# Banded attention's scores from whole 128-row operands: both parts of a head's q stacked in one tile, both parts of k twice

## The chip, the cores and the metric

One core of a Trainium2 chip runs the whole kernel in one launch. The metric is the device time of one execution in microseconds. The engines are TensorE (PE, with its weight loads PEld), VectorE (DVE), ScalarE (ACT), GpSimd (POOL) and SyncE (SP, which here only issues transfers).

## The reference

The kernel computes the trunk of a hybrid encoder: 2 layers, 512 tokens, 1024 channels, all in fp32. Each layer projects the tokens once for two token mixers and their gates, runs mixer A (banded grouped-query attention), mixer B (three groups of dilated banded attention), merges them by gates, and goes on with a projection, a LayerNorm, a squared-ReLU MLP, a gated per-layer embedding and another LayerNorm. What matters here is mixer A:

```python
A_Q_HEADS, A_KV_HEADS, HEAD_DIM, A_WINDOW = 8, 2, 64, 128
qa = _rope(qa.reshape(bsz, seq, A_Q_HEADS, HEAD_DIM), cos, sin)    # rotary, first 16 of 64 channels
ka = _rope(ka.reshape(bsz, seq, A_KV_HEADS, HEAD_DIM), cos, sin)
oa, _ = _banded_attention(qa, ka, va, A_WINDOW, a_sink)

def _banded_attention(q, k, v, window, sink=None):
    ...
        s = jnp.einsum('nqkgd,nskd->nkgqs', qj.astype(jnp.float32) * scale, kj)
        ...
        s = jnp.where(mask, s, -jnp.inf)          # |i - j| <= 128
        m = jnp.maximum(jnp.max(s, axis=-1), sink_b)
        e = jnp.exp(s - m[..., None])
        denom = jnp.sum(e, axis=-1) + jnp.exp(sink_b - m)
        o = jnp.einsum('nkgqs,nskd->nqkgd', e, vj) / denom
```

A query block of 128 tokens sees its own block and its two neighbours: 256 keys at the ends of the sequence and 384 inside.

## The kernel before

**Products in two parts.** TensorE multiplies a reduced form of fp32. Each operand is therefore split in two: hi, the operand rounded to that form (a copy by ACT, L222), and lo, what is left (a subtraction by DVE, L223). A product takes three passes, hi·hi, lo·hi and hi·lo, which add up in one PSUM bank (`mm3`, L272 to L276). Weights arrive in fp32 by DMA (`wst`) and are split the same way into `whi` and `wlo`, 128x1024 at a time, in three buffers each.

**Channels on partitions.** q and k lie with the channel on the partition, two heads of 64 channels to a tile of 128 rows and 512 tokens. The four q tiles of mixer A hold heads i and i + 4, which use the two heads of the one k tile. `rope` (L365) turns a projection into such a tile: DVE shuffles the partitions of a PSUM bank (L368), DVE multiplies the bank by the cosines (L369), POOL multiplies the shuffled tile by the sines (L370), DVE adds (L371), and ACT and DVE split the sum (L222, L223) into a `qh` and a `ql` tile, of which there are 5 each for q and k of both mixers.

**The scores.** `pair_scores` (L429) makes the scores of one query block for the two heads of a tile: three passes, in each of which the two heads' matmuls follow one another, one on rows 0 to 63 and one on rows 64 to 127, into two PSUM banks. They are named sa, in mixer B sb. DVE then adds the mask and takes the maximum in one custom instruction (`masked`, L426), ACT exponentiates (L422), PE transposes the probabilities (`probs_T`, L411), ACT and DVE split them (ptha, ptla), and PE multiplies them with the values (`weighted`, L437 and L438) into the one bank oa. A head's sum leaves that bank by a copy of ACT and an addition of DVE (`join`, L442 and L443: fa); PE spreads the reciprocal denominators (L456: rsa), DVE scales (L457) and splits into oah and oal.

**PSUM.** There are 3 banks for projections (mm), 2 for scores (s), 2 for transposes (pt) and 1 for outputs (o). The next use of a bank waits until its last reader is done with it.

**The order of the work.** PE's order in the attention is the one in which the code emits it, under a manual schedule; the code that emits it is a planner (L802 to L835). It goes round: first the ready steps of up to two units (`unit_a` for a q tile of mixer A, `unit_b` and `mix_b` for mixer B), else one step of the filler (`filler`, L746), that is 3 matmuls of a projection listed in FLOW (L34): q tiles 2 and 3 of mixer A, the gates (g), q, k and v of mixer B (qb, kb, vb), and later the branch products. Whether a step is ready it asks a small model of time (`Forecast`, L162): each PE step books its length, `fc.on` books times on ACT, DVE and POOL, and the banks carry the time at which they come free. A score group books 6w/2400 us there, w being its columns. The order on DVE, ACT, POOL and SP is set by a scheduler that sees all instructions.

**Constants.** Cosines, sines, the masks and an identity come as one array. A layer loads all but the identity by one DMA into a tile of 1920 columns (L344 to L353), the identity by another one in layer 0.

Of the kernel before, what the change touches and what calls it, by code (L numbers as in the profile page):

```python
# [20 lines left out]
P = 128  # L21
# [110 lines left out]
CONST_COLS = [("cos", S), ("sin", S), ("ma", 384), ("m0", 256), ("m1", P), ("m2", P), ("id", P)]  # L132


def shape_constants():
# [23 lines left out]
    return np.concatenate([c, s, ma, m0, m1, m2, np.eye(P, dtype=np.float32)], axis=1)  # L159
# [40 lines left out]
def build(nc, tc, plan, down, xT, xN, pT, wst, vec, rows, sink, cst, out):  # L200
# [3 lines left out]
    with ctx:  # L204
# [138 lines left out]
        def attention_block(l, av, rp, vt, OA, OB, begun):  # L343
            ct = rp.tile([P, cst.shape[1] - P], F32, tag="ct", name=f"ct{l}", bufs=1)  # L344
            cc, off = {}, 0
            for n, w in CONST_COLS[:-1]:
                cc[n] = ct[:, off:off + w]
                off += w
# [16 lines left out]
            def rope(ps, dil, name):  # L365
# [6 lines left out]
                hi = av.tile([P, S], F32R, tag="qh", name="qh" + name, bufs=5)  # L372
                lo = av.tile([P, S], F32R, tag="ql", name="ql" + name, bufs=5)
# [60 lines left out]

            def weighted(o, vv, blk, r, pT, cols, first, last):
# [30 lines left out]
            def unit_a(i):  # L466
                q, k = held["qa", i], held["ka"]
# [8 lines left out]
                for j in range(4):  # L476
# [4 lines left out]
                    pair_scores(ss, q, k, slice(j * P, (j + 1) * P), slice(k0, k1), slice(0, w))  # L481
                    fc.pe(6 * w / 2400)
# [8 lines left out]
                held["free_qk"] += 1 + (i == 3)  # L491
# [221 lines left out]
            held = {"P": 0, "qk": 3, "free_qk": 0, "vv": 0}  # L713
# [6 lines left out]
            held["ka"] = rope(kps, False, f"ka{l}")  # L720
# [3 lines left out]
            held["qa", 0] = rope(q0, False, f"qa{l}_0")  # L724
            fc.take("mm")
            held["qa", 1] = rope(q1, False, f"qa{l}_1")
# [19 lines left out]
            def filler():  # L746
                def project(key, sigma_order):
# [3 lines left out]
                    held[key] = rope(ps, sigma_order, "_".join(str(v) for v in (l, *key)))  # L751

                for kind, *idx in FLOW:
                    if kind == "qa":
                        yield from project(("qa", *idx), False)
# [27 lines left out]
            def slots(n, *keys):  # L783
                def ok():
                    if held["P"] + n > 4 or any(k not in held or fc.t < held[k][2] for k in keys):
                        return False
# [546 lines left out]
```

## Time and profile before

| | |
|---|---|
| median of 3 runs | 1546.28 us (1545.49 to 1547.36) |
| the profiled execution | 1546.11 us, its span 1544.3 us |
| busy in the span | PE 1512.5 us, DVE 1091.1, ACT 714.9, POOL 201.3 |
| score matmuls of mixer A (L433, sa) | 192 in both layers, 64 rows each, 256 or 384 columns |
| mixer A's units in layer 0 | about 29 to 118 us of the span |
| mixer A's units in layer 1 | from about 797 us |

The page gives for each engine the time in which it was busy, and the trace the single instructions. In the rows of the timeline stand start, busy time, engine, line, operation, output and inputs by their names, the shape, how many instructions the row holds, and in brackets the idle time ahead of it with what ended it. Matmuls overlap: their busy time is longer than the distance from one to the next, so what a matmul costs PE is read from the starts. In the rows of the waits stand the instruction that waited, the one it waited for, the time in all, how often, and the longest wait.

### The profile page before, as it was taken

Reading aid. Unit: us, or ns where it says so; the run is one execution under the profiler, and the core shown is the slowest. Engines: PE = TensorE matmul, PEld = TensorE weight load, DVE = VectorE, ACT = ScalarE, POOL = GpSimd, SP = SyncE. Lnnn points to the kernel's source line nnn. Section 1 sums busy time; section 2 is a strip of 40 time slices with the busy share of each in tenths; the row PEclk is TensorE's granted clock in tenths of the full one; section 3 lists DMA queues with packets and bytes.
Section 4 is the critical chain, followed back from the end, with each engine's and each line's share of the span. In section 5 each row is a group of like instructions: output and inputs, shape, how many; then the busy total and the mean of one; then the engine's idle time right before and its main releaser. Section 6 shows DMA issues by size and latency. Waiting matters only on the chain.

```text
span 1544.3 us, 19518 instructions
## 1 busy us (share of the span) xinstructions
PE 1512.5 (98%) x7416; PEld 1241.6 (80%) x7416; DVE 1091.1 (71%) x1809; ACT 714.9 (46%) x1186; POOL 201.3 (13%) x159
## 2 busy tenths in 40 slices
PE   8999999999999999999999999999999999999996
PEld 6778788888888888888887778888888888888885
DVE  6778675457568767696877786744575776767868
ACT  4566554344334443444546665543442443444342
POOL 1111110020011120202010101111100211111021
PEclk9999999999999999999999999999999999999998
DMA  6211224245622415142342121255456233241403
GB/s 219 69 55 56 69 69 167 85 127 161 194 71 81 145 49 161 44 151 68 96 149 68 56 69 56 81 164 148 134 140 207 68 98 121 71 134 55 150 1 95
DMA packets 46317, 162.19 MB, mean 105 GB/s; under 512 B 5648, under 2 KB 5776, under 8 KB 46224
## 3 DMA queue, kind: packets, MB, share of 16 engines
q1 hardware_dynamic: 43200, 152.00, 30.7%
q0 software_dynamic: 2448, 8.91, 3.1%
q8 instruction: 58, 0.95, 0.3%
q14 instruction: 35, 0.29, 0.1%
q10 hardware_dynamic: 576, 0.04, 0.0%
HBM read 155.16 MB, written 4.19 MB: 103 GB/s over the span
## 4 chain that ended last, share of the span: by engine, by line
PE 89%; DVE 6%; ACT 2%; DMA 2%; issue 1%; SPq 0%; ACTq 0%; DVEq 0%
PE dn L1004 17%; PE ps_up L275 8%; PE ps_up L274 8%; PE ps_up L276 8%; PE wo L281 2%; PE wo L282 2%; PE wo L280 2%; PE pg L282 2%; PE pg L281 2%; PE pg L280 2%; DVE wlo L223 1%; PE sa L433 1%; PE sb L433 1%; PE pta L411 1%; PE ps_start L274 1%
## 5 line engine op out<-in xcount | busy, mean ns | idle before, releaser
L223 DVE TENSOR_TENSOR wlo<-wst,whi 128x1024 fp32r<-128x1024 f32 (+1 forms) x171 | 220.2, 1291 | 149.5 <-ACT whi L222 144.8
L222 ACT CAST whi<-wst 128x1024 fp32r<-128x1024 f32 (+1 forms) x171 | 175.5, 1026 | 295.2 <-PE ps_up L275 115.5
L274 PE MATMUL ps_up<-xhi,whi 128*128 128x512 f32 x512 | 199.2, 389 | 0.0
L275 PE MATMUL ps_up<-xlo,whi 128*128 128x512 f32 x512 | 199.2, 389 | 0.0
L276 PE MATMUL ps_up<-xhi,wlo 128*128 128x512 f32 x512 | 199.2, 389 | 0.0
L977 POOL TENSOR_TENSOR hr<-r 128x512 f32<-128x512 f32 x64 | 102.2, 1597 | 551.4 <-ACT r L969 531.0
L274 PEld LDWEIGHTS ps_up<-xhi,whi 128*128 128x128 f32 x512 | 96.1, 188 | 20.0
L276 PEld LDWEIGHTS ps_up<-xhi,wlo 128*128 128x128 f32 x512 | 96.1, 188 | 20.0
L275 PEld LDWEIGHTS ps_up<-xlo,whi 128*128 128x128 f32 x512 | 96.1, 188 | 19.9
L222 ACT CAST whi<-raw 128x1024 fp32r<-128x1024 f32 x56 | 58.0, 1052 | 97.0 <-PE ps_up L275 57.6
L222 ACT CAST dhi<-raw 128x1024 fp32r<-128x1024 f32 x56 | 58.7, 1052 | 81.9 <-PE dn L1004 60.0
L1023 DVE TENSOR_TENSOR y<-y,dn 128x512 f32<-128x512 f32 x96 | 65.1, 682 | 38.7 <-PE dn L1004 38.7
L957 DVE TENSOR_TENSOR raw<-raw,raw 128x1024 f32<-128x1024 f32 x64 | 86.4, 1349 | 0.2
L223 DVE TENSOR_TENSOR wlo<-raw,whi 128x1024 fp32r<-128x1024 f32 x56 | 68.2, 1221 | 14.1 <-ACT whi L222 14.1
L223 DVE TENSOR_TENSOR dlo<-raw,dhi 128x1024 fp32r<-128x1024 f32 x56 | 69.2, 1239 | 5.4 <-ACT dhi L222 5.2
L1004 PE MATMUL dn<-whi,smh 128*128 128x512 f32 x128 | 50.1, 394 | 0.7 <-DVE y L1023 0.7
L282 PE MATMUL pg<-bhi,xlo 128*128 128x512 f32 x128 | 49.9, 390 | 0.9 <-DVE xlo L901 0.9
L1004 PE MATMUL dn<-wlo,smh 128*128 128x512 f32 x128 | 50.6, 395 | 0.2
L1004 PE MATMUL dn<-whi,sml 128*128 128x512 f32 x128 | 49.9, 390 | 0.0
L280 PE MATMUL pg<-bhi,xhi 128*128 128x512 f32 x128 | 49.9, 390 | 0.0
L1004 PE MATMUL dn<-dhi,smh 128*128 128x512 f32 x128 | 49.9, 390 | 0.0
L1004 PE MATMUL dn<-dlo,smh 128*128 128x512 f32 x128 | 49.8, 389 | 0.0
(834 smaller groups left out, 3878.4 us busy)
## 6 DMA issues: line engine op xcount, KB each, us to landing
wst<-wst SPq DMA_DIRECT2D x187, 512.0 KB, 3.6
raw<-wst SPq DMA_DIRECT2D x64, 512.0 KB, 4.3
y<-rows POOLq DMA_DIRECT2D x14, 512.0 KB, 7.8
row<-rows SPq DMA_DIRECT2D x7, 512.0 KB, 9.4
wst<-wst SPq DMA_DIRECT2D x10, 256.0 KB, 3.6
xs<-xT SPq DMA_DIRECT2D x8, 256.0 KB, 5.0
y<-xN SPq DMA_DIRECT2D x4, 512.0 KB, 6.2
kept<-y SPq DMA_DIRECT2D x4, 512.0 KB, 2.8
```

Of the source, the lines that this page charges most:

```text
L222: nc.scalar.copy(hi, src)
L223: nc.vector.tensor_tensor(lo, src, hi.bitcast(F32), ALU.subtract)
L274: nc.tensor.matmul(ps, w[0][:, s], x[0], start=start, stop=False, skip_group_check=part)
L275: nc.tensor.matmul(ps, w[0][:, s], x[1], start=False, stop=False, skip_group_check=part)
L276: nc.tensor.matmul(ps, w[1][:, s], x[0], start=False, stop=stop, skip_group_check=part)
L280: nc.tensor.matmul(ps, x[0], w[0][:, c], start=start, stop=False)
L281: nc.tensor.matmul(ps, x[0], w[1][:, c], start=False, stop=False)
L282: nc.tensor.matmul(ps, x[1], w[0][:, c], start=False, stop=stop)
L957: nc.vector.tensor_tensor(to, to, other, ALU.add)
L977: nc.gpsimd.tensor_tensor(h.rearrange("p s t -> p (s t)"), r, r, ALU.mult)
L1004: nc.tensor.matmul(ps[s], a[:, k, tok], w[b][:, cols], start=first and not (k or m), stop=k == 3 and m == 2, skip_group_check=True)
L1023: return nc.vector.tensor_tensor(to, to, ps, ALU.subtract if n in (2, 4, 5) else ALU.add)
```

## The change

The scores of mixer A no longer pair two heads of 64 rows. For each head, q is kept as one tile of 128 rows that holds the hi part in one half and the lo part in the other half, and k as two tiles, the hi part in both halves and the lo part in both halves. One matmul with k's hi tile gives hi·hi + lo·hi, a second one with k's lo tile gives hi·lo and also lo·lo, which was left out before. So a group takes 4 matmuls of 128 rows (`whole_scores`) in place of 6 of 64 rows. Mixer B still uses `pair_scores`.

For that, `rope` splits the rotated tile in pieces of 64 rows: a q tile by 2 pieces on ACT and 2 on DVE in place of 1 and 1, the k tile by 4 and 4 in place of 1 and 1. The planner books 4w/2400 us for a group, the rotation's steps for such tiles by the table ROPE, and the buffers of `qh` and `ql` go from 5 to 6, with the limit in the filler. The constants lie in four tiles that share the 12 buffers of the gates (11 before): four DMAs in place of one, each layer. In the changed kernel the lines of the attention stand 37 to 42 further on: L426 is L463, L433 is L475, L437 and L438 are L479 and L480, L411 is L448, L368 is L376, L369 is L377, L371 is L379, L456 and L457 are L498 and L499, L442 and L443 are L484 and L485.

```diff
-CONST_COLS = [("cos", S), ("sin", S), ("ma", 384), ("m0", 256), ("m1", P), ("m2", P), ("id", P)]
+CONST_COLS = [[("cos", S)], [("sin", S)], [("ma", 384), ("m1", P)], [("m0", 256), ("m2", P)], [("id", P)]]
...
-            ct = rp.tile([P, cst.shape[1] - P], F32, tag="ct", name=f"ct{l}", bufs=1)
+                ct = rp.tile([P, S], F32, tag="gate", name=f"ct{l}_{i}", bufs=12)
+                cts.append((ct[:, :n], cst[:, off:off + n]))
...
             def load_constants():
-                nc.sync.dma_start(ct, cst[:, :off])
+                for to, what in cts:
+                    nc.sync.dma_start(to, what)
...
-            def rope(ps, dil, name):
+            def rope(ps, dil, name, whole=""):
+                ROPE = (0.6, 0.6, 1.23, 0.48)
...
+                if whole:
+                    a = fc.on("dve", ROPE[0], fc.t + HOP)
+                    b = fc.on("dve", ROPE[1], a)
+                    c = fc.on("pool", ROPE[2], a + HOP)
+                    fc.give("mm", b + HOP)
+                    t = fc.on("dve", ROPE[1], max(b, c) + HOP) + HOP
+                    half = [t1[0:64], t1[64:P]]
+                    if whole == "q":
+                        both = pair()
+                        for r, x in enumerate(both):
+                            own, other = (slice(r * 64, r * 64 + 64), slice(64 - r * 64, P - r * 64))
+                            nc.scalar.copy(x[own], half[r])
+                            nc.vector.tensor_tensor(x[other], half[r], x[own].bitcast(F32), ALU.subtract)
+                            u = fc.on("dve", ROPE[1], fc.on("act", ROPE[3], t) + HOP) + HOP
+                        return both, u
+                    both = [pair(0), pair(1)]
+                    for r, (hi, lo) in enumerate(both):
+                        own, other = (slice(r * 64, r * 64 + 64), slice(64 - r * 64, P - r * 64))
+                        nc.scalar.copy(hi[own], half[r])
+                        nc.vector.tensor_tensor(lo[own], half[r], hi[own].bitcast(F32), ALU.subtract)
+                        nc.vector.tensor_tensor(lo[other], half[r], hi[own].bitcast(F32), ALU.subtract)
+                        nc.scalar.copy(hi[other], half[r])
...
+            def whole_scores(ss, q, k, qs, ks, col):
+                for r in range(2):
+                    for n in range(2):
+                        nc.tensor.matmul(ss[r][:, col], q[r][:, qs], k[r][n][:, ks], start=n == 0, stop=n == 1)
...
-                    pair_scores(ss, q, k, slice(j * P, (j + 1) * P), slice(k0, k1), slice(0, w))
-                    fc.pe(6 * w / 2400)
+                    whole_scores(ss, q, k, slice(j * P, (j + 1) * P), slice(k0, k1), slice(0, w))
+                    fc.pe(4 * w / 2400)
...
-                held["free_qk"] += 1 + (i == 3)
+                held["free_qk"] += 1 + 2 * (i == 3)
...
-                    yield lambda: held["qk"] - held["free_qk"] < 5
+                    yield lambda: held["qk"] - held["free_qk"] < 6
```

The change also moves instructions. PE's order of layer 0 before, from the last score matmul of query block 2 of the first q tile (sa0_0_2) on to the first of block 3 (sa0_0_3); the names are output, inputs and shape:

```order
L433 MATMUL sa0_0_2_1_466<-qhka0_285,qlqa0_0_298 128x384
L274 MATMUL ps_0_('qa', 3)_430<-xhi_72,whi6_327 128x512
L275 MATMUL ps_0_('qa', 3)_430<-xlo_73,whi6_327 128x512
L276 MATMUL ps_0_('qa', 3)_430<-xhi_72,wlo6_328 128x512
L274 MATMUL ps_0_('g', 0, 1)_497<-xhi_72,whi7_368 128x512
L275 MATMUL ps_0_('g', 0, 1)_497<-xlo_73,whi7_368 128x512
L276 MATMUL ps_0_('g', 0, 1)_497<-xhi_72,wlo7_369 128x512
L274 MATMUL ps_0_('g', 0, 1)_497<-xhi_72,whi7_368 128x512
L275 MATMUL ps_0_('g', 0, 1)_497<-xlo_73,whi7_368 128x512
L276 MATMUL ps_0_('g', 0, 1)_497<-xhi_72,wlo7_369 128x512
L433 MATMUL sa0_0_3_0_504<-qhka0_285,qhqa0_0_297 128x256
```

And the same place now:

```order
L276 MATMUL ps_0_('g', 0, 1)_491<-xhi_72,wlo7_389 128x512
L475 MATMUL sa0_0_2_0_529<-qh0ka0_291,qhqa0_0_311 128x384
L475 MATMUL sa0_0_2_0_529<-ql0ka0_292,qhqa0_0_311 128x384
L475 MATMUL sa0_0_2_1_530<-qh1ka0_293,qlqa0_0_312 128x384
L475 MATMUL sa0_0_2_1_530<-ql1ka0_294,qlqa0_0_312 128x384
L475 MATMUL sa0_0_3_0_540<-qh0ka0_291,qhqa0_0_311 128x256
L475 MATMUL sa0_0_3_0_540<-ql0ka0_292,qhqa0_0_311 128x256
L475 MATMUL sa0_0_3_1_541<-qh1ka0_293,qlqa0_0_312 128x256
L475 MATMUL sa0_0_3_1_541<-ql1ka0_294,qlqa0_0_312 128x256
L274 MATMUL ps_0_('qb', 0, 0)_564<-xhi_72,whi8_438 128x512
```

Before, products of the filler (of q tile 3 and a gate) stand between the two groups; now the groups stand directly behind one another, and the filler's q projection of mixer B (qb) comes behind both.

DVE at this place now, from the rotation's sum of q tile 3 on; the two rows L396 are the pieces of that tile, the rows L463 the masks:

```order
L379 TENSOR_TENSOR t10_qa_3_474<-t10_qa_3_474,sw0_qa_3_473 128x512
L529 SCALAR_TENSOR_TENSOR nma0_0_414<-mxa0_0_413,nsk0_148 128x2
L396 TENSOR_TENSOR qh0_qa_3_479<-t10_qa_3_474,qh0_qa_3_479 64x512
L396 TENSOR_TENSOR ql0_qa_3_480<-t10_qa_3_474,ql0_qa_3_480 64x512
L463 ISA pa0_0_0_411,mxa0_0_413<-sa0_0_2_0_529,ct0_2_144 128x384
L463 ISA mxa0_0_413 128x1
L463 ISA pa0_0_1_412,mxa0_0_413<-sa0_0_2_1_530,ct0_2_144 128x384
L463 ISA mxa0_0_413 128x1
L529 SCALAR_TENSOR_TENSOR nma0_0_414<-mxa0_0_413,nsk0_148 128x2
L463 ISA pa0_0_0_411,mxa0_0_413<-sa0_0_3_0_540,ct0_2_144 128x256
L463 ISA mxa0_0_413 128x1
```

The masks of block 2 stand behind the two pieces, and the first of block 3 directly behind them.

The second place is PE around the end of the first q projection of mixer B, qb(0,0). Before, from the transposes pta0_0_3 to the value products on ptha0_0_2 and ptla0_0_2:

```order
L411 MATMUL pta0_0_3_600<-ident_64,pa0_0_1_380 128x128 x4
L274 MATMUL ps_0_('qb', 0, 0)_617<-xhi_72,whi8_426 128x512
L275 MATMUL ps_0_('qb', 0, 0)_617<-xlo_73,whi8_426 128x512
L276 MATMUL ps_0_('qb', 0, 0)_617<-xhi_72,wlo8_427 128x512
L433 MATMUL sa0_1_2_0_621<-qhka0_285,qhqa0_1_307 128x384
L433 MATMUL sa0_1_2_1_622<-qhka0_285,qhqa0_1_307 128x384
L433 MATMUL sa0_1_2_0_621<-qlka0_286,qhqa0_1_307 128x384
L433 MATMUL sa0_1_2_1_622<-qlka0_286,qhqa0_1_307 128x384
L433 MATMUL sa0_1_2_0_621<-qhka0_285,qlqa0_1_308 128x384
L433 MATMUL sa0_1_2_1_622<-qhka0_285,qlqa0_1_308 128x384
L437 MATMUL oa0_0_0_585<-ptha0_0_2_594,vvva0_322 128x384
L438 MATMUL oa0_0_0_585<-ptla0_0_2_595,vvva0_322 64x384
```

There the filler's matmuls of qb(0,0) stand ahead of these products. Now PE reads, from four value products behind the end of qb(0,0) on:

```order
L448 MATMUL pta0_0_2_633<-ident_64,pa0_0_0_411 128x128 x3
L479 MATMUL oa0_0_0_628<-ptha0_0_1_601,vvva0_340 128x384
L480 MATMUL oa0_0_0_628<-ptla0_0_1_602,vvva0_340 64x384
L448 MATMUL pta0_0_3_643<-ident_64,pa0_0_1_412 128x128 x4
L475 MATMUL sa0_1_2_0_652<-qh0ka0_291,qhqa0_1_323 128x384
L475 MATMUL sa0_1_2_0_652<-ql0ka0_292,qhqa0_1_323 128x384
L475 MATMUL sa0_1_2_1_653<-qh1ka0_293,qlqa0_1_324 128x384
L475 MATMUL sa0_1_2_1_653<-ql1ka0_294,qlqa0_1_324 128x384
L479 MATMUL oa0_0_0_628<-ptha0_0_2_637,vvva0_340 128x384
L480 MATMUL oa0_0_0_628<-ptla0_0_2_638,vvva0_340 64x384
```

Between the transposes into pta0_0_2 and the value products on ptha0_0_2 and ptla0_0_2 no matmul of a projection is left.

DVE around the split ptla0_0_2 and the masks of sa0_1_2 (rows L426), before:

```order
L426 ISA pa0_1_1_408,mxa0_1_409<-sa0_1_1_1_573,ct0_142 128x384
L426 ISA mxa0_1_409 128x1
L223 TENSOR_TENSOR wlo10_614<-wst10_611,whi10_613 128x1024
L487 SCALAR_TENSOR_TENSOR nma0_1_410<-mxa0_1_409,nsk0_145 128x2
L223 TENSOR_TENSOR ptla0_0_2_595<-pta0_0_2_590,ptha0_0_2_594 128x384
L223 TENSOR_TENSOR ptla0_0_3_606<-pta0_0_3_600,ptha0_0_3_605 128x512
L426 ISA pa0_1_0_407,mxa0_1_409<-sa0_1_2_0_621,ct0_142 128x384
L426 ISA mxa0_1_409 128x1
L426 ISA pa0_1_1_408,mxa0_1_409<-sa0_1_2_1_622,ct0_142 128x384
```

There the weight split wlo10 stands two rows ahead of ptla0_0_2. DVE now, with masks in the rows L463:

```order
L223 TENSOR_TENSOR ptla0_0_1_602<-pta0_0_1_597,ptha0_0_1_601 128x384
L376 STREAM_SHUFFLE sw0_qb_0_0_663<-ps_0_('qb', 0, 0)_564 128x512
L377 TENSOR_TENSOR t10_qb_0_0_664<-ps_0_('qb', 0, 0)_564,ct0_0_142 128x512
L223 TENSOR_TENSOR wlo11_706<-wst11_703,whi11_705 128x1024
L223 TENSOR_TENSOR ptla0_0_2_638<-pta0_0_2_633,ptha0_0_2_637 128x384
L463 ISA pa0_1_0_449,mxa0_1_451<-sa0_1_2_0_652,ct0_2_144 128x384
L463 ISA mxa0_1_451 128x1
L379 TENSOR_TENSOR t10_qb_0_0_664<-t10_qb_0_0_664,sw0_qb_0_0_663 128x512
```

Now ptla0_0_2 stands behind a shuffle and a cosine product of qb(0,0) and the weight split wlo11.

The third place is PE behind the projection qb(0,1), now, from the last matmul of that projection on:

```order
L276 MATMUL ps_0_('qb', 0, 1)_978<-xhi_72,wlo12_800 128x512
L448 MATMUL pta0_2_1_1052<-ident_64,pa0_2_0_770 128x128 x3
L479 MATMUL oa0_2_0_1060<-ptha0_2_0_1022,vvva0_340 128x256
L480 MATMUL oa0_2_0_1060<-ptla0_2_0_1023,vvva0_340 64x256
L479 MATMUL oa0_2_0_1060<-ptha0_2_0_1022,vvva0_340 128x256
L480 MATMUL oa0_2_0_1060<-ptla0_2_0_1023,vvva0_340 64x256
L448 MATMUL pta0_2_2_1065<-ident_64,pa0_2_0_770 128x128 x3
L475 MATMUL sa0_3_2_0_1083<-qh0ka0_291,qh0_qa_3_479 128x384
L475 MATMUL sa0_3_2_0_1083<-ql0ka0_292,qh0_qa_3_479 128x384
L475 MATMUL sa0_3_2_1_1084<-qh1ka0_293,ql0_qa_3_480 128x384
L475 MATMUL sa0_3_2_1_1084<-ql1ka0_294,ql0_qa_3_480 128x384
L479 MATMUL oa0_2_0_1060<-ptha0_2_1_1056,vvva0_340 128x384
```

No matmul of a projection stands between these products. DVE there now, from the shuffle of qb(0,1) on:

```order
L376 STREAM_SHUFFLE sw0_qb_0_1_1073<-ps_0_('qb', 0, 1)_978 128x512
L377 TENSOR_TENSOR t10_qb_0_1_1074<-ps_0_('qb', 0, 1)_978,ct0_0_142 128x512
L223 TENSOR_TENSOR wlo15_1138<-wst15_1135,whi15_1137 128x1024
L463 ISA pa0_3_0_997,mxa0_3_999<-sa0_3_2_0_1083,ct0_2_144 128x384
L463 ISA mxa0_3_999 128x1
L223 TENSOR_TENSOR ptla0_2_1_1057<-pta0_2_1_1052,ptha0_2_1_1056 128x384
L463 ISA pa0_3_1_998,mxa0_3_999<-sa0_3_2_1_1084,ct0_2_144 128x384
L463 ISA mxa0_3_999 128x1
L223 TENSOR_TENSOR ptla0_2_2_1070<-pta0_2_2_1065,ptha0_2_2_1069 128x384
```

The split ptla0_2_1, which PE's last row needs, stands on DVE behind the shuffle, the cosine product, a weight split and a mask.

More of the change, by code (lines that the diff above doesn't have):

```diff
@@ L371, in rope, with pair @@
                 nc.vector.tensor_tensor(t1, t1, sw, ALU.add)
[L372 to L373 removed]
+                def pair(n=""):
+                    return [av.tile([P, S], F32R, tag="q" + e, name=f"q{e}{n}{name}", bufs=6) for e in "hl"]
+                if whole:
[20 more added lines that the diff above has]
+                        nc.scalar.copy(hi[other], half[r])
+                        u = fc.on("act", ROPE[3], t)
+                        fc.on("act", ROPE[3], u)
+                        u = fc.on("dve", 2 * ROPE[1], u + HOP) + HOP
+                    return both, u
+                hi, lo = pair()
                 if dil:
```

33 lines of the change are left out of this document (18 added, 15 removed).

## The prediction

> **What bounds the kernel now.** I read the page's table of engines first, then busy time by stretch, then the waits.
>
> ```profile
> PE 1512.5 (98%) x7416; PEld 1241.6 (80%) x7416; DVE 1091.1 (71%) x1809; ACT 714.9 (46%) x1186; POOL 201.3 (13%) x159
> ```
>
> TensorE is busy for 98 % of the span, so only two things move the end: the time its instructions take, and the few places where it waits. The stretch of layer 0 in which mixer A begins (columns: start and end, length, busy time per engine with counts, the clock granted to TensorE):
>
> ```profile
> 29.00:58.00 29.00, 28.25 (x140) 21.33 (x138) 25.90 (x57) 14.89 (x35) 5.95 (x5) 1.00 0.26 76
> ```
>
> PE is near full at clock 1.00. VectorE (DVE, third) has only 29.00 − 25.90 = 3.1 us free. What PE waits for in layer 0's attention, from 29 to 256 us:
>
> ```profile
> PE vtvb L401 <- ACT vTvb L387: 1.5, 1, 1.5
> PE pta L411 <- ACT pa L422: 1.1, 2, 0.6
> PE ob L438 <- DVE ptlb L223: 0.8, 1, 0.8
> PE rs L456 <- ACT wide L450: 0.7, 2, 0.4
> PE ob L646 <- DVE ogb L443: 0.7, 1, 0.7
> ```
>
> 4.8 us in all; 1.1 (pta) lies before 118 us, in the stretch that changes most, and 3.7 behind it. So an order of the work exists in which PE hardly waits; the change alters that order, and I count what it puts in its place.
>
> **The score groups: a gain.** A group is one 128-row block of queries against its band, both heads of a tile. The 512-column products ahead of it show PE's pace:
>
> ```profile
> 44.22 0.39 PE L275 MATMUL ps_('qa', 3)_430<-xlo,whi 128*128 128x512 f32 x1
> 44.45 0.39 PE L276 MATMUL ps_('qa', 3)_430<-xhi,wlo 128*128 128x512 f32 x1
> 44.76 0.45 PE L433 MATMUL sa<-qhka,qhqa 64*128 64x384 f32 x2
> 45.05 0.34 PE L433 MATMUL sa<-qlka,qhqa 64*128 64x384 f32 x2
> 45.22 0.33 PE L433 MATMUL sa<-qhka,qlqa 64*128 64x384 f32 x2
> ...
> 45.83 0.40 PE L275 MATMUL ps_('qa', 3)_430<-xlo,whi 128*128 128x512 f32 x1
> ```
>
> One product takes 0.2275 from start to start (44.22 to 44.45). From 44.45 to 45.83 are 1.38 us with two such products in them, so the group costs 1.38 − 0.455 = 0.925. The same for a 256-column group:
>
> ```profile
> 50.56 0.39 PE L276 MATMUL ps_('g', 0, 1)_497<-xhi,wlo 128*128 128x512 f32 x1
> ...
> 51.77 0.39 PE L275 MATMUL ps_('g', 0, 1)_497<-xlo,whi 128*128 128x512 f32 x1
> ```
>
> 1.21 − 0.455 = 0.755. The two heads of a pass run together (a pair of 384 columns starts 0.17 after the one before, 45.05 to 45.22); the rest, 0.925 − 3 × 0.17 = 0.42, is paid around the group, where PE goes from 128 rows to 64 and back. After the change a group is four products of 128 rows, one behind the other. Their price by 256-column rows of that kind:
>
> ```profile
> 782.18 0.28 PE L275 MATMUL ps_start<-xlo,whi 128*128 128x256 f32 x1
> 782.30 0.28 PE L276 MATMUL ps_start<-xhi,wlo 128*128 128x256 f32 x1
> ```
>
> 0.12 each, so 4 × 0.12 = 0.48; for 384 columns 0.17 each (between 0.12 and 0.2275), 0.70. The gain is 0.925 − 0.70 = 0.225 and 0.755 − 0.48 = 0.275, eight groups of each kind per layer: 1.8 + 2.2 = **4.0 us per layer, 8.0 in all**.
>
> [...]
>
> **The added splits on DVE and ACT: a cost.** Per layer k takes 4 + 4 pieces of 64x512 in place of 1 + 1 of 128x512, and each of four q tiles 2 + 2: seven more on DVE and seven more on ACT. On DVE (start, busy time):
>
> ```profile
> 107.27 0.42 DVE L426 CUSTOM_DVE_ANT_0 pa<-sa,ct 128x256 f32<-128x256 f32 x1
> ...
> 107.61 0.68 DVE L443 TENSOR_TENSOR fa<-oa,fa 64x512 f32<-64x512 f32 x1
> 108.21 0.54 DVE L223 TENSOR_TENSOR ptla<-pta,ptha 128x384 fp32r<-128x384 f32 x1
> ```
>
> A 64x512 piece takes 0.60 until the next starts (107.61 to 108.21), so 7 × 0.60 = 4.2 us; all of it falls into the stretch quoted at the beginning, where 3.1 are free. ACT has 29.00 − 14.89 = 14.1 us free there, and I take its seven at nothing. For the first group nothing is lost:
>
> ```profile
> 35.37 0.68 DVE L223 TENSOR_TENSOR qlka<-t1ka,qhka 128x512 fp32r<-128x512 f32 x1
> ...
> 36.82 0.39 PE L433 MATMUL sa<-qhka,qhqa 64*128 64x256 f32 x2
> ```
>
> DVE reaches its first piece at 35.37; the four of k and two of q end at 35.37 + 6 × 0.61 = 39.03. The new order puts the group 12 products later, at 36.82 + 12 × 0.2275 = 39.55. That cover is 0.5 us.
>
> **The moved order: new waits, the dearest term.** The planner now books 4w/2400 per group instead of 6w/2400, and reserves the rotation's steps on DVE and POOL. In the new order value products and transposes follow the end of a q or k fill without the fill work that stood between them. They need DVE, and there, at the end of each fill, stand the shuffle, the cosine product and the next weights' split:
>
> ```profile
> 77.91 0.74 DVE L368 STREAM_SHUFFLE sw_kb<-ps_('kb', 0, 0)_718 128x512 f32<-128x512 f32 x1
> 78.54 0.68 DVE L369 TENSOR_TENSOR t_kb<-ps_('kb', 0, 0)_718,ct 128x512 f32<-128x512 f32 x1
> ...
> 78.79 1.29 POOL L370 TENSOR_TENSOR sw_kb<-sw_kb,ct 128x512 f32<-128x512 f32 x1 [6.88 <-DVE sw_kb L368]
> ...
> 79.38 1.78 DVE L223 TENSOR_TENSOR wlo<-wst,whi 128x1024 fp32r<-128x1024 f32 x1 [0.17 <-ACT whi L222]
> 81.09 0.55 DVE L223 TENSOR_TENSOR ptla<-pta,ptha 128x384 fp32r<-128x384 f32 x1
> 81.55 0.68 DVE L371 TENSOR_TENSOR t_kb<-t_kb,sw_kb 128x512 f32<-128x512 f32 x1
> ```
>
> This burst takes 81.09 − 77.91 = 3.18 us, the split 1.78 of it beside POOL's sine product. Once it ran at full pace while POOL was the slow one:
>
> ```profile
> 109.56 2.76 POOL L370 TENSOR_TENSOR sw_qb<-sw_qb,ct 128x512 f32<-128x512 f32 x1 [7.42 <-DVE sw_qb L368]
> ...
> 109.97 1.22 DVE L223 TENSOR_TENSOR wlo<-wst,whi 128x1024 fp32r<-128x1024 f32 x1
> 111.10 1.24 DVE L492 TENSOR_TENSOR sea<-nma,nsk 128x8 f32<-128x8 f32 x1
> ```
>
> There the split took 1.13 (109.97 to 111.10), and the burst would be 0.63 + 0.59 + 1.13 = 2.35. These are my two bounds, 3.18 and 2.35. [...]
>
> The other steps. DVE: a 384-column mask by
>
> ```profile
> 48.59 0.56 DVE L426 CUSTOM_DVE_ANT_0 pa<-sa,ct 128x384 f32<-128x384 f32 x1 [0.54 <-PE sa L433]
> 49.07 0.08 DVE L426 DVE_READ_ACCUMULATOR2_ANT mxa<- 128x1 f32 x1
> ```
>
> 0.48, of 256 columns 0.34 (107.27 to 107.61); a split of 384 columns 0.46 (81.09 to 81.55); sums and 512-column splits 0.60 as the piece above. PE: two value products of 384 columns and four transposes by
>
> ```profile
> 59.64 0.42 PE L437 MATMUL oa<-ptha,vvva 128*128 128x384 f32 x1
> ...
> 60.08 0.60 PE L411 MATMUL pta<-ident,pa 128*128 128x128 f32 x4
> 60.43 0.48 PE L274 MATMUL ps_('qb', 0, 0)_617<-xhi,whi 128*128 128x512 f32 x1
> ```
>
> 0.44 and 0.35 (three: 0.26); four value products of 256 columns 4 × 0.12 = 0.48; three fill products 0.68. With T as the end of a fill, DVE starting its burst 0.2 after it (a product is busy 0.39 and the next starts after 0.23, so its result lies 0.16 behind), both bounds of each wait:
>
> 1. sa0_0_3 stands directly behind sa0_0_2 (12 fill products less between): it needs a score bank, freed by a mask that queues behind two of the new pieces. At most both pieces, 2 × 0.60 = 1.2. At least: the first head's products 0.35, a mask 0.48, and 0.2 to each side between the engines, 1.23, less the 0.70 that PE is busy, 0.5.
> 2. Behind qb(0,0), the value products on ptla0_0_2: PE at T + 0.48 + 0.26 + 0.44 + 0.35 + 0.70 = T + 2.23; DVE at T + 0.2 + burst + 0.46 = T + 3.84 or 3.01. Wait 1.6 or 0.8.
> 3. sa0_1_3's second bank: on DVE mask, sum, split, mask 0.48 + 0.60 + 0.60 + 0.48 = 2.16; PE 0.44 + 0.26 + 0.24 = 0.94. Wait 1.2.
> 4. Behind kb(0,0), oa0_1_0 needs the one output bank, freed by a sum behind the burst and two masks: DVE T + 0.2 + burst + 0.68 + 0.60 = T + 4.66 or 3.83; PE T + 0.44 + 0.35 + 0.48 + 0.68 + 0.26 + 0.68 = T + 2.89. Wait 1.8 or 0.9.
> 5. pta0_1_2 needs the bank of the scaling (L456, L457): DVE sum, split, scaling and a small one 1.76, PE 1.16. Wait 0.6.
> 6. Behind qb(0,1), the products on ptla0_2_1: PE T + 0.26 + 0.48 + 0.26 + 0.70 = T + 1.70; DVE T + 0.2 + burst + 0.48 + 0.46 = T + 4.32 or 3.49. Wait 2.6 or 1.8.
> 7. Behind kb(0,1), oa0_3_0's output bank: DVE T + 0.2 + burst + 0.60 = T + 3.98 or 3.15; PE about T + 2.7, with its two 64-row groups. Wait 1.3 or 0.4.
>
> They come to 10.3 or 6.2 per layer. Each wait also lets DVE catch up, and rows of both kinds occur, so I take the middle, 8.25.
>
> **The constants.** At nothing: layer 0 still loads them while its first products run. In layer 1 the four transfers now stand among the stores at the layer's end, beside weights that POOL fetches (the stretch of the DMA view from 764 to 770 us, its last column the time to landing, and the timeline):
>
> ```profile
> DMA packets 375, 1.44 MB, mean 240 GB/s; under 512 B 25, under 2 KB 25, under 8 KB 374
> ...
> wlo<-wst POOLq DMA_DIRECT2D x1, 512.0 KB, 6.5
> ```
>
> ```profile
> 764.78 0.86 POOL L229 DMA_DIRECT2D wlo<-wst  x1 [7.11 <-ACT wlo L228]
> ...
> 773.80 0.28 PE L276 MATMUL ps_start<-xhi,wlo 128*128 128x256 f32 x1
> ```
>
> They land at 764.78 + 6.5 = 771.3 and are needed at 773.8, 2.5 later. The constants are 1792 columns, 0.92 MB: wholly ahead of them at 240 GB/s that is 3.8 us, so 1.3 late at most, 0 at least. I take 0, since transfers share rather than queue.
>
> **Sum.** Per layer +8.25 (new waits) − 4.0 (groups) − 1.1 (the pta waits that go with the old order) = +3.15; both layers have the same order on PE, so +6.3. The profiled execution took 1546.11, 0.2 under the median, nearer than the runs agree among themselves. 1546.1 + 6.3 = **1552.4 us**. With 6.2 and 10.3 of new waits it is +2.2 and +10.4: 1548.3 to 1556.5, and 1557.8 with the constants' 1.3.
>
> **The rivals.**
> - *Faster: the stalls are their own cure.* Each wait gives DVE and ACT a lead, and the 3.7 us of waits behind 118 us go. With the lower bound 6.2 − 4.0 − 4.8 = −2.6 per layer: 1540.9; with no new waits either, −8.8 per layer: 1528.5, too far to be likely since waits 3 and 5 hang on no burst (they alone leave −8.8 + 1.8 = −7.0: 1532.1). For it: PE's margin between work and waits is small everywhere. Against it: the later waits stand on rows of mixer B (vtvb, ob) that the change leaves as they are. It decides from new waits under 8.8 − 1.6 = 7.2 per layer (1.6 is half of the 0.2 % below), if the later ones go. Chance 0.27.
> - *No change.* New waits of 5.1 per layer, half of the upper count, eat exactly 4.0 + 1.1, with the later waits as they were: 1546.1. Chance 0.14.
> - *Slower for another reason: packing lost.* If groups of 64 rows cost only 3 × 0.17 = 0.51 and 3 × 0.12 = 0.36, four products of 128 rows would add 0.19 and 0.12 each, 2.5 per layer, 1551 without any wait. The 0.925 and 0.755 above speak against it. Chance 0.03.
>
> **How the numbers follow.** Forecast with its bounds 0.56, rivals 0.27, 0.14 and 0.03. A measurement of this kernel can tell about 0.2 %, 3.1 us, from no change: faster 0.27, same 0.14, slower 0.59 (0.56 + 0.03). The range must reach into the faster case to hold eight in ten: from 1540 (just under 1540.9) to 1558, the upper end of the forecast; the forecast alone would have 1548.3 to 1557.8.
>
> **What would show it.** Right: PE's groups at L475 0.70 and 0.48 between the fill products; in the waits of PE, rows for L475 and L480 behind DVE's L463, L223 and L485 with 6 to 10 us up to some 125 us; DVE's bursts at the ends of qb and kb fills with PE idle behind them. Wrong: groups that cost as before, less than 5 us of such waits per layer, or mixer B's waits gone.

## The result, and the profile after

The changed kernel takes 1565.32 us (1563.53 to 1566.83, 4 runs) where the kernel before took 1546.57 beside it: a ratio of 1.0121, interval 1.0108 to 1.0133, 18.8 us slower. The forecast was 1552.4 with a range from 1540 to 1558. The direction is as forecast, the size three times as large, and the time lies above the range. The profiled execution took 1564.66 us with a span of 1562.9, 18.6 more than before. From here on all differences of profiles are between spans.

The page's table of engines, of the changed kernel:

```profile
PE 1513.5 (97%) x7352; PEld 1249.4 (80%) x7352; DVE 1102.6 (71%) x1823; ACT 724.5 (46%) x1200; POOL 201.6 (13%) x159
```

PE is busy for the same time as before (1512.5) with 64 instructions fewer, and for a smaller share: the span grew by idle time. What PE waits for in the whole span, in the changed kernel (in all, how often, longest):

```profile
PE oa L480 <- DVE ptla L223: 7.2, 4, 2.3
PE oa L479 <- DVE fa L485: 6.0, 4, 1.8
PE ps_start L274 <- ACT whi L222: 5.0, 1, 5.0
PE sa L475 <- DVE mxa L463: 4.5, 4, 1.3
PE sa L475 <- DVE t1qa L377: 2.4, 1, 2.4
PE pta L448 <- DVE ptla L223: 2.0, 2, 1.0
PE dn L1046 <- DVE y L1065: 1.9, 4, 0.8
PE ob L480 <- DVE ptlb L223: 1.6, 2, 0.8
PE rs L498 <- ACT wide L492: 1.5, 4, 0.4
PE vtvb L438 <- ACT vTvb L424: 1.0, 2, 0.5
PE pg L282 <- DVE xlo L943: 1.0, 1, 1.0
PE ps_('qa', 3)_6921 L274 <- DVE t1qa L377: 0.7, 1, 0.7
PE sb L470 <- DVE ql_kb L223: 0.5, 1, 0.5
```

These are 35.3 us. Before there were 17.9: twice the 4.8 quoted in the prediction (9.8 with the second layer's own numbers) and, elsewhere, these rows of the kernel before:

```profile
PE ps_start L274 <- ACT whi L222: 5.7, 1, 5.7
...
PE dn L1004 <- DVE y L1023: 1.5, 4, 0.4
...
PE pg L282 <- DVE xlo L901: 0.9, 1, 0.9
```

So 17.4 of the 18.6 us look like waits. That is not yet the sum, because the groups did become cheaper. A 384-column group of the changed kernel between two products, in the timeline of PE:

```profile
104.77 0.34 PE L475 MATMUL sa<-qh0ka,qh_qa 128*128 128x384 f32 x1
104.95 0.34 PE L475 MATMUL sa<-ql0ka,qh_qa 128*128 128x384 f32 x1
105.13 0.33 PE L475 MATMUL sa<-qh1ka,ql_qa 128*128 128x384 f32 x1
105.30 0.34 PE L475 MATMUL sa<-ql1ka,ql_qa 128*128 128x384 f32 x1
105.47 0.39 PE L274 MATMUL ps_('qb', 0, 1)_978<-xhi,whi 128*128 128x512 f32 x1
```

105.47 − 104.77 = 0.70, the number of the prediction. Summed over the starts around all 16 groups of layer 1, with what the neighbours lose by them, they took some 14 us before and take some 11 now: about 3.0 less per layer, 6.0 in all. This is an estimate, uncertain by about half a microsecond per layer, since the usual distance of the neighbours has to be taken from other places. Something else must cost about as much as the groups saved, and it shows in the clock. The table of stretches around the first of three places where it fell (length, busy times of PE, PEld, DVE, ACT, POOL, then the granted clock):

```profile
42.00:45.00 3.00, 3.00 (x10) 2.30 (x9) 2.90 (x8) 2.40 (x4) 0.00 (x0) 0.54 0.31 120
45.00:48.00 3.00, 3.00 (x13) 2.49 (x12) 2.59 (x3) 2.69 (x7) 0.00 (x0) 0.89 0.16 59
```

The first drop is worth (0.46 + 0.11) × 3.00 = 1.71 us of lost clock, as if PE ran at half clock for 3.42 us. The second, from 113.94 us on, and a third one, in layer 1 from 905.83 on, are as large (their rows stand in the last section): 5.1 us in all. Before, no stretch of the attention is below 1.00. In all three cases PE had just stood idle: behind a wait of 2.40 us, behind one of 2.27, and behind two of 1.22 and 1.00 that lie close together.

The sum now: +17.4 waits, +5.1 clock, −6.0 for the groups, 16.5 of 18.6. The rest, 2.1, lies, as far as rows show it, around the waits: at 112.67 below, the two products are 112.67 − 110.03 = 2.64 apart, the counted wait is 2.27, and two such products are 0.17 to 0.26 apart without a wait, so 0.1 to 0.2 is lost besides. The changed kernel has eleven counted waits more (31 against 20); at 0.1 to 0.2 each they would lose 1.1 to 2.2. This is an estimate from one row, and no run shows the 2.1 as such.

The dearest single wait is the sixth of the prediction. PE's timeline:

```profile
110.03 0.38 PE L479 MATMUL oa<-ptha,vvva 128*128 128x384 f32 x1
112.67 0.39 PE L480 MATMUL oa<-ptla,vvva 128*64 128x384 f32 x1 [2.27 <-DVE ptla L223]
```

and DVE's and POOL's at that time:

```profile
108.42 0.75 DVE L376 STREAM_SHUFFLE sw_qb<-ps_('qb', 0, 1)_978 128x512 f32<-128x512 f32 x1
109.05 0.68 DVE L377 TENSOR_TENSOR t_qb<-ps_('qb', 0, 1)_978,ct 128x512 f32<-128x512 f32 x1
109.64 2.03 DVE L223 TENSOR_TENSOR wlo<-wst,whi 128x1024 fp32r<-128x1024 f32 x1
111.60 0.55 DVE L463 CUSTOM_DVE_ANT_0 pa<-sa,ct 128x384 f32<-128x384 f32 x1
...
112.07 0.55 DVE L223 TENSOR_TENSOR ptla<-pta,ptha 128x384 fp32r<-128x384 f32 x1
```

```profile
109.31 1.28 POOL L378 TENSOR_TENSOR sw_qb<-sw_qb,ct 128x512 f32<-128x512 f32 x1 [27.43 <-DVE sw_qb L376]
```

The burst is 111.60 − 108.42 = 3.18 us, the prediction's upper bound to the digit; the split took 2.03 beside POOL's product of 1.28. Behind it come a mask and then the split that PE waits for.

### The profile page after: what moved, and what is told of

It reads as the page before. It is cut to its first block, busy times and chain, and to the rows that moved or that the text cites. A ratio compares the mean times of both kernels' runs of the same rounds, so it can differ in the third digit from the quotient of the medians.

```text
span 1562.9 us, 19433 instructions
## 1 busy us (share of the span) xinstructions
PE 1513.5 (97%) x7352; PEld 1249.4 (80%) x7352; DVE 1102.6 (71%) x1823; ACT 724.5 (46%) x1200; POOL 201.6 (13%) x159
## 4 chain that ended last, share of the span: by engine, by line
PE 84%; DVE 9%; issue 3%; ACT 2%; DMA 1%; POOL 0%; SPq 0%; DVEq 0%; POOLq 0%; ACTq 0%
PE dn L1046 16%; PE ps_up L276 7%; PE ps_up L275 7%; PE ps_up L274 7%; PE pg L282 2%; PE wo L280 2%; PE wo L282 2%; PE wo L281 2%; PE pg L281 2%; PE pg L280 2%; DVE wlo L223 2%; PE ps_start L274 1%; PE sb L470 1%; PE ps_start L275 1%; PE ps_start L276 1%
## 5 line engine op out<-in xcount | busy, mean ns | idle before, releaser
L223 DVE TENSOR_TENSOR wlo<-wst,whi 128x1024 fp32r<-128x1024 f32 (+1 forms) x171 | 224.9, 1318 | 155.5 <-ACT whi L222 150.9
L1046 PE MATMUL dn<-dhi,sml 128*128 128x512 f32 x128 | 49.8, 389 | 0.0
```

What stands on the lines that cost most here:

```text
L223: nc.vector.tensor_tensor(lo, src, hi.bitcast(F32), ALU.subtract)
L1046: nc.tensor.matmul(ps[s], a[:, k, tok], w[b][:, cols], start=first and not (k or m), stop=k == 3 and m == 2, skip_group_check=True)
```

## The experiments

All runs are compared with the kernel before on the same chip.

| run | median, us | ratio to before | interval |
|---|---|---|---|
| the changed kernel | 1565.32 | 1.0121 | 1.0108 to 1.0133 |
| new_order | 1572.18 | 1.0168 | 1.0143 to 1.0192 |
| old_order | 1552.10 | 1.0034 | 1.0024 to 1.0043 |
| constants | 1546.78 | 0.9998 | 0.9989 to 1.0008 |
| one_split | 1561.49 | 1.0087 | 1.0067 to 1.0107 |
| late_start | 1545.76 | 0.9992 | 0.9983 to 1.0001 |
| act_copies | 1543.87 | 0.9981 | 0.9973 to 0.9990 |
| book6 | 1561.19 | 1.0090 | 1.0075 to 1.0104 |
| rotation_booked_as_before | 1573.39 | 1.0177 | 1.0163 to 1.0191 |
| split_booked_late | 1560.78 | 1.0087 | 1.0072 to 1.0103 |
| stalls | 1565.64 | 1.0122 | 1.0107 to 1.0136 |
| short_stalls | 1554.99 | 1.0055 | 1.0038 to 1.0071 |

My theory was that the order costs the time (the order theory); the rival, that the seven added pieces per layer make DVE late in whatever order (the load theory).

**Order and work crossed.** The planner's loop of one kernel was replaced by the list of its moves in the other ("+" starts a unit, "f" is a step of the filler, a digit a step of a unit), which gives the old work in the new order and the new work in the old one. A line with the list makes the line numbers of these kernels one higher: L476 is L475 of the changed kernel, L438 and L439 are L437 and L438 of the one before.

```diff
-                while waiting or live or side or fill:
+                for move in ORDER:
+                    if move == "+":
                         key = next(iter(waiting))
+                        live[key] = [waiting.pop(key)[1](), None]
+                    elif move == "f":
+                        try:
+                            next(fill)
...
```

> The kernel before with its 64-row score groups and old splits, but PE's steps emitted in the changed kernel's order. Order theory: the waits on ptla and fa behind the ends of qb and kb are there, some 7 us per layer, with one or more drops of the granted clock: 1558 to 1564 us. Load theory: without the added pieces there is little to wait for, 1546 to 1550.

> The changed kernel with its new score groups and all its split pieces, but PE's steps emitted in the order of the kernel before. Order theory (the waits come from the order that the planner's new bookings give): the waits on ptla, fa and the score banks between 50 and 125 us go; the groups save about 3.4 us per layer; the first group, which stands earlier again, waits up to 5 us for its pieces in layer 0 and 1 in layer 1. 1543 to 1547 us. Load theory (the seven added pieces per layer make DVE late, in whatever order): most of the 20 us of new waits stay, 1556 or more.

The old work in the new order takes 1572.18 us, worse than the changed kernel. Its waits in layer 0 (29 to 300 us) are the predicted ones, without one added piece in the kernel:

```profile
PE oa L439 <- DVE ptla L224: 4.4, 3, 1.8
PE oa L438 <- DVE fa L444: 2.4, 2, 1.2
PE sa L434 <- DVE mxa L427: 2.0, 2, 1.3
PE pta L412 <- DVE ptla L224: 1.0, 1, 1.0
```

So the order alone costs 25.8 us (1572.18 against 1546.41 beside it), and the load theory falls as the main cause. It overshot my 1558 to 1564: the clock fell at three places, at one of them for twice as long, for which I had allowed one or more. In that order the new work is worth 1572.18 − 1565.32 = 6.9 us, in spans 1569.4 − 1562.9 = 6.5, pieces and all. Of the 6.5, 1.7 are the one stretch at half clock that the changed kernel does not have, while its counted waits are 2.4 longer (35.3 against 32.9), so the groups themselves come to 6.5 − 1.7 + 2.4 = 7.2 by this count: between the 6.0 read from the starts and the 8.0 of the prediction.

The new work in the old order takes 1552.10, not the 1543 to 1547 expected. The waits behind qb and kb are gone, but the first group now waits in layer 0 for:

```profile
PE sa L476 <- DVE t1qa L378: 2.8, 1, 2.8
PE sa L476 <- DVE qhqa L397: 2.0, 1, 2.0
```

Here the load does count: 4.8 us, with a drop of the clock behind it that is twice as long. The profiled execution, the slowest of ten, also has two drops in layer 1, behind waits of 2.0 us (on qhqa) and 1.6 us.

**The pieces and the constants alone.**

```diff
-                        for r, x in enumerate(both):
-                            own, other = ...
-                            nc.scalar.copy(x[own], half[r])
-                            nc.vector.tensor_tensor(x[other], half[r], x[own].bitcast(F32), ALU.subtract)
+                        split(both[0], both[1], t1)
...
+                        one = pair(0)
+                        split(one[0], one[1], t1)
+                        both = [one, one]
```

> The changed kernel in its own order of PE's steps, with each rotated tile of mixer A split by one operation on ACT and one on DVE as before, so that the score groups read whole hi and lo tiles and the scores are other numbers: it leaves out the building of the stacked tiles. Order theory: only the waits at the first group (2.4 us in layer 0) and behind the pieces in sa0_0_3 (up to 0.6 per layer) go, with the drop of the clock that follows the first: 1558 to 1562 us. Load theory: the waits go with the pieces, 1540 to 1550.

1561.49: 3.8 us of the 18.8 belong to the pieces (the two ratios' intervals leave anything from 0.2 to 10), as expected by the order theory. The 2.4 us at the first group are gone; the waits on ptla and fa are, to the digit, those of the changed kernel (3.6 and 3.0 per layer).

The constants (the diff of the constants above, put into the kernel before):

> The kernel before with only its constants in four tiles among the gates' buffers and four DMAs. Order theory and load theory: nothing of the 18.8 us, at most the 1.1 us that the changed kernel lost between the layers: 1546.5 to 1547.6 us. A theory that the transfers matter: 1549 or more, with waits at the start of layer 1.

1546.78, no difference.

**What the planner was told.** Each of the new bookings was put back alone; put back together, they give the old order, move for move.

```diff
-                    fc.pe(4 * w / 2400)
+                    fc.pe(6 * w / 2400)
```

> The changed kernel with only the planner's booking of a score group put back to 6w/2400 us. If the smaller booking moved the work: the order and with it the time come back towards the old order, 1545 to 1553 us. If the new bookings of the rotation moved it: the waits stay, 1558 to 1568 us.

```diff
-                            u = fc.on("dve", ROPE[1], fc.on("act", ROPE[3], t) + HOP) + HOP
-                        return both, u
+                        return both, forecast_split(S, t - HOP)[1] + HOP
```

> The changed kernel with only the planner's bookings of the rotation put back to those of before; a score group is still booked 4w/2400 us. With both put back the planner gives the old order word for word, so this and the run with 6w/2400 split the blame. If the rotation's bookings alone made the bad order: 1550 to 1554 us, as in the old order. If the group's booking alone gives it too, from the second q tile on: the waits behind qb(0,0) may go, those behind kb(0,0), qb(0,1) and kb(0,1) stay, with the first group's 4.8 us: 1558 to 1567 us.

1561.19 and 1573.39, the second above both times expected: either booking alone leads to an order with long waits, so the blame can't be split. I then told the planner of the burst:

```diff
                 w = weights(key)
-                fc.on("dve", 1.135, fc.on("act", 0.947, fc.t + HOP) + HOP)
...
                     yield None
+                fc.on("dve", 1.78, fc.on("act", 0.947, fc.t + HOP) + HOP)
                 return ps
...
-            fc.take("s", 3.5)
+            fc.take("s", 13.0)
```

> The changed kernel with its own bookings, but the planner now books the next weights' split where the chip does it, at the end of a projection and with 1.78 us on DVE instead of 1.135 at its beginning, and takes the score bank of q tile 1's projection to be held for 13 us instead of 3.5. If the waits come from a planner that does not know of the burst on DVE: most of the waits behind the ends of qb and kb go, and the one at the first group: 1543 to 1553 us. If any order of this work waits as much: 1558 or more.

1560.78, with 4.7 us of waits on score banks and 3.8 on fa in layer 0. So it is not shown that the planner's ignorance of the burst makes the bad order; it stays open which knowledge would give a good one. Four of its orders were measured for this work, and all four are 14 to 27 us slower than the kernel before.

**Repairing the order.** The new work in the old order, with its first group behind 8 more steps of the filler (4 more matmul steps than in the changed kernel), the next ones two later:

```diff
-ORDER = "0ff0fffffffffff+00fff+1fffffffff0fff0ffff00fff100fff10000fff100ffffff1...
+ORDER = "0ff0fffffffffffffffffffff+00fff+1f0fff0ffff00fff100fff10000fff100ffff1...
```

> The changed kernel's work in the old order of PE's steps, but with the first score group behind 8 more steps of the filler (41 us instead of 36 in layer 0), where the pieces and the cosine product of q tile 1 are done, and the next groups two steps later. Order theory: the 4.8 us of waits at the first group of layer 0 and the 2.0 in layer 1 go, and the drops of the granted clock behind them; what is left is the groups' saving of about 3.4 us per layer: 1540 to 1544 us, faster than both kernels. Load theory (the pieces' time on DVE comes back somewhere): 1548 or more.

1545.76, above the 1540 to 1544 expected, and not told apart from before. Its profiled execution, 3 us above this median, has one drop of the clock, at 517 us, behind a wait of 2.7 us outside the attention. A wait of 1.6 us on a score bank and 1.0 on ptla in layer 0 were left: the mask queues behind four pieces. Therefore two pieces per layer went to ACT:

```diff
-                        nc.vector.tensor_tensor(lo[other], half[r], hi[own].bitcast(F32), ALU.subtract)
+                        nc.scalar.copy(lo[other], lo[own].bitcast(F32))
```

> The kernel of the late first group, with the second copies of k's lo parts made by ACT from the first ones, which takes two of the seven added pieces per layer, 1.4 us, off DVE. If DVE's load is what is left of the loss in that order: the wait of 1.6 us on a score bank shrinks or goes, 1541 to 1545 us, faster than the kernel before. If the load no longer matters there: 1545 to 1547.

1543.87, faster than both kernels (0.9981 of before). What the two pieces alone are worth is not told apart, since the intervals of this run and of late_start overlap. But the wait on the score bank in layer 0 shrank:

```profile
PE oa L481 <- DVE ptla L224: 1.0, 1, 1.0
PE sa L476 <- DVE mxa L464: 0.9, 1, 0.9
```

**What a wait costs beyond itself.** In the kernel before, in its own order, PE was made to wait by a late copy on ACT:

```diff
+STALL = {(0, 1): 1, (0, 2): 3, (1, 1): 2, (1, 2): 5}
...
+                for x in first:
+                    nc.scalar.copy(wide.rearrange("p j r d -> p (j r d)"), x)
                 nc.scalar.copy(wide, c.rearrange("p r (j u) -> p j r u", u=1).to_broadcast([P, 4, 2, 64]))
```

> The kernel before in its own order, with four stalls of PE put in: at the scaling of units 1 and 2 of each layer PE waits for a copy on ACT that comes behind 1, 3, 2 and 5 needless copies of 0.6 us. Clock theory (an idle PE loses half of its clock for some 3.4 us afterwards where the idle time takes about half of such a stretch, at a price of some 1.6 us each): the longer stalls, over 2 us, are followed by stretches at a granted clock of 0.5, the shortest may not be; the time grows by the added idle time plus 1.3 to 1.7 us for each drop. Plain theory (a wait costs its own length and no more): no drop, and the time grows by the idle time alone.

The time rose by 18.5 us, with four waits of 2.1, 4.3, 2.7 and 5.9 us, 14.9 in all, less the two waits on vtvb of 3.0 that went: 11.9. These rows are those of the slowest of the four executions (1569.25, 22.1 above): there the clock fell behind each of the four waits, behind the longest for two stretches, five times 1.71 or 8.5 us, which with the 11.9 makes 20.4 of the 22.1. Behind the shortest, which ends at 98.3:

```profile
96.00:99.00 3.00, 0.93 (x8) 0.54 (x8) 1.08 (x4) 2.19 (x6) 0.00 (x0) 1.00 0.00 0
99.00:102.00 3.00, 3.00 (x15) 2.44 (x16) 2.82 (x8) 2.29 (x4) 0.00 (x0) 0.69 0.04 8
102.00:105.00 3.00, 3.00 (x15) 1.92 (x14) 1.70 (x6) 1.31 (x5) 0.00 (x0) 0.74 0.44 135
```

Again (0.31 + 0.26) × 3.00 = 1.71. The plain theory (a wait costs its length) falls. The same with shorter waits:

```diff
-STALL = {(0, 1): 1, (0, 2): 3, (1, 1): 2, (1, 2): 5}
+STALL = {(0, 1): 1, (0, 2): 1, (1, 1): 1, (1, 2): 1}
...
-                    nc.scalar.copy(wide.rearrange("p j r d -> p (j r d)"), x)
+                    nc.scalar.copy(wide[:, 0, 0, :], x[:, 0:64])
```

> The same four stalls made shorter: the copy on ACT comes behind one copy of 64 columns and the copy of the join, so that PE waits some 1.3 to 1.8 us each time instead of 2.1 to 5.9. Clock theory: idle times under half of 3.4 us are followed by no drop of the granted clock, or by one of the four at most; the time grows by the added idle time, less some 3 us of later waits that go: 1548 to 1552 us. If any wait of over 1 us costs clock: four drops and 1554 or more.

1554.99: a time as in the second forecast, but with two drops, not four, and so as neither of the two said. The waits are 1.68, 1.77, 1.67 and 2.05 us, with a drop behind the first and the last and none behind the other two. So 1.7 us can be enough, or not; where the wait falls in time decides, as the last section shows.

## Why the prediction was right or wrong, point by point

The mechanism was right: the moved order makes new waits that cost more than the cheaper groups save. What failed are terms of the sum. The largest is the price of a wait: its length alone, with nothing for the clock behind it (measured 5.1 us). The first group was put at nothing (2.4 us of waiting), the seven waits midway between their bounds (16.5, measured 19.7), and the gain at 8.0 (about 6.0).

- **What bounds the kernel, the price of a group.** Right where a group stands between projections, as the 0.70 shows. The gain was about 6.0 by the starts, not 8.0. Behind transposes a group of 384 columns takes 0.78 (67.39 to 68.17 by PE's timeline), and what is left of a group of 256 columns behind a wait takes longer too (834.83 to 835.65, 0.82 in place of 0.48); those I had not priced.
- **The new waits.** Right in mechanism, place and, mostly, size. In layer 0: the first 0.77 (forecast 0.5 to 1.2; 1.34 in layer 1), the second 1.35 (0.8 to 1.6), the third 1.18 (1.2), the fourth 1.79 (0.9 to 1.8), the sixth 2.27 (1.8 to 2.6), the seventh 1.21 (0.4 to 1.3). The fifth did not come at pta0_1_2; a wait of 1.00 came two units later, at transposes behind the seventh. Together 9.6 and, in layer 1, 10.2, against 8.25 and the bounds of 6.2 and 10.3. The middle was the wrong choice: in the burst shown above the split took 2.03 us beside POOL's product, and at qb(0,0), by DVE's timeline,

```profile
67.32 2.02 DVE L223 TENSOR_TENSOR wlo<-wst,whi 128x1024 fp32r<-128x1024 f32 x1
```

  2.02, beside POOL's product again (66.98 to 68.26): at both places the burst is the long one. Why it was not the one of 2.35, no run shows.
- **The first group at nothing, with 0.5 us of cover.** Wrong. I followed the pieces, which ended in time: on DVE the last one of q starts at 37.78. But the second head's bank still held the projection of q tile 1, and its cosine product comes later on DVE:

```profile
37.78 0.69 DVE L396 TENSOR_TENSOR qlqa<-t1qa,qlqa 64x512 fp32r<-64x512 f32 x1
...
39.15 1.23 DVE L223 TENSOR_TENSOR wlo<-wst,whi 128x1024 fp32r<-128x1024 f32 x1
40.29 0.68 DVE L377 TENSOR_TENSOR t1qa<-ps_start,ct 128x512 f32<-128x512 f32 x1
```

  In the kernel before, it ran ahead of q's lo part,

```profile
36.08 0.69 DVE L369 TENSOR_TENSOR t1qa<-ps_start,ct 128x512 f32<-128x512 f32 x1
36.69 0.69 DVE L223 TENSOR_TENSOR qlqa<-t1qa,qhqa 128x512 fp32r<-128x512 f32 x1
```

  and now it stands behind the pieces and the next weights' split. PE waited 2.4 us, and lost 1.7 of clock behind it. The cover for the pieces was small as well: PE reached the group at 38.33 and not at 39.55, and the last piece ended at 38.47. The step that I missed is whose bank the group needs, not only which operands.
- **The waits that go.** I took 1.1 per layer. All 2.2 of pta went, and also 2.1 of vtvb and the 1.4 of ob behind ogb: the faster rival's mechanism is real, but worth 1.8 per layer and not the 3.7 that it needed.
- **The wait's price.** Wrong, and the largest omission: I priced a wait at its length. Three drops of the granted clock cost 5.1 us. Around the waits some 2.1 more seem to be lost, which is argued and not shown.
- **Constants.** Right: nothing. That transfers share shows in the changed kernel, in the DMA view from 774.5 to 775 us: POOL's weights took 9.2 us to land and the first tile of constants, issued behind them, 4.8 beside them; PE has no wait from 765 to 800 us.
- **Packing lost** (the rival in which the pairs of 64 rows, 0.17 apart, are the cheaper form). Refuted: in the new order the new work is cheaper than the old by 6.9 us; in the old order it is dearer (1552.10), but no longer once its first group stands later (1545.76).

From forecast to measurement: +3.2 for the seven waits (19.7 − 16.5), +3.6 for waits not foreseen (2.4 and 0.7 on t1qa, 0.5 on ql_kb), +5.1 clock, +2.1 of the rest, +2.0 of gain that was missing, −3.5 of further waits that went: 12.5, and 18.8 − 6.3 is 12.5. That it closes to the digit is chance: the smaller waits outside the attention, which differ by a few tenths, are not in it.

## What to carry to other kernels

Where PE is full, a cheaper instruction is worth only what the order leaves of it: keep the order by hand first, change the work in it, and let a planner reorder only afterwards, since its parameters may fit one set of costs. List for each early instruction not only its operands but who last used its PSUM bank, and what stands ahead of that reader in its queue. Price a wait of PE at its length, and add the 1.7 us that a drop of the clock cost here where PE's idle time, of one wait or of several close together, may come to half of one of the stretches of 3.41 us that the next section shows.

## What the hardware showed that I had not expected

Each drop of the clock that can be read from windows of 3 us is 1.71 us of lost clock, that is 3.42 us at 0.50, or twice as long (3.39 to 3.42 us of lost clock). Where they lie says more: in every profiled run with several drops these begin whole multiples of 3.413 us apart (in the changed kernel at 42.26, 113.94 and 905.83: 21 of them and then 232), so a trace can be cut into the stretches by which the clock changes. Some of them in the changed kernel, with PE's busy time as the first after the length:

```profile
110.52:113.94 3.42, 1.26 (x8) 1.04 (x9) 3.42 (x8) 0.34 (x1) 0.24 (x3) 1.00 0.38 109
113.94:117.35 3.41, 3.41 (x13) 2.95 (x12) 3.27 (x9) 3.36 (x8) 0.00 (x0) 0.50 0.11 44
...
885.35:888.76 3.41, 2.24 (x16) 1.84 (x14) 3.15 (x4) 2.12 (x5) 1.46 (x3) 1.00 0.00 0
888.76:892.18 3.42, 2.32 (x16) 2.04 (x17) 3.42 (x11) 1.37 (x3) 0.00 (x0) 1.00 0.46 156
892.18:895.59 3.41, 3.41 (x18) 2.84 (x17) 2.96 (x9) 3.38 (x11) 0.00 (x0) 1.00 0.01 2
902.42:905.83 3.41, 1.66 (x9) 1.18 (x10) 3.38 (x12) 0.72 (x1) 0.00 (x0) 1.00 0.52 159
905.83:909.24 3.41, 3.41 (x19) 2.49 (x18) 2.65 (x6) 3.20 (x11) 0.00 (x0) 0.50 0.00 0
```

In layer 0 the wait of 2.27 us lies almost whole in one stretch, which leaves PE 1.26 us busy, and the next stretch runs at 0.50. In layer 1 an edge at 888.76 cuts the same wait in two: PE is busy for 2.24 and 2.32, and no drop follows. The two waits of 1.22 and 1.00 us fall mostly into one stretch (1.66 busy) and are followed by a drop, though neither is long. In the short stalls it is the same: 1.68 and 1.81 us of idle time in one stretch were followed by a drop, while the waits of 1.77 and 1.67, each cut in two by an edge, left at most 0.94 in a stretch.

In the changed kernel the stretches ahead of its three drops leave PE idle for 2.28, 2.16 and 1.75 us, and no other stretch from 10 to 1540 us for more than 1.62 (858.03 to 861.44, PE busy for 1.79); in the kernel before, the most is 1.52 (897.02 to 900.43, busy for 1.89), with no drop behind it. Of the other runs, cut in the same way, the stalls have a drop behind 1.56 us (in the stretch that ends at 100.14) and the short stalls behind 1.68 (at 97.44), while late_start has none behind 1.65 (from 46.2 on). So about half of the 3.41 us was enough, and from 1.56 to 1.68 both were seen. Behind a stretch at half clock less was enough to stay there: 0.65 us of idle time in rotation_booked_as_before (from 75.00 us on), about 0.4 in book6 (from 846.8 on). With none, as in the row of 113.94, the clock came back. It fits that behind the wait of 5.9 us (idle for the whole stretch from 902.25 to 905.66 and for 1.0 of the next) two stretches at half clock follow one another.
